# Attention: keys loaded once beside doubled queries, queries asked for ahead of values, first loads moved in memory, bias rows in one transfer

## The chip, the cores and the metric

One core of a Trainium2 chip runs the whole program in one launch. The metric is the device time of a run in microseconds (us), as a median over runs. Engines are named as the profile names them: PE (matmul), PEld (its weight load), DVE (VectorE), ACT (ScalarE), POOL (GpSimd), and SP, which here only starts DMAs. Every engine works through its own instructions in program order, so an instruction that waits holds back all that stand behind it on the same engine.

## The reference, cut to what matters

Two layers of a transformer block over 2048 latent tokens and 256 context tokens, width 1024. In each layer one input projection feeds three head groups: six query heads with two key heads in a window of 128 tokens (called A here), a short convolution, and six heads of two-dimensional neighbourhood attention with a relative position bias (called C). An output projection and a mixture of 16 experts follow. The parts that the change touches are the logits of A and C:

```
s_win = einsum('bnqkgd,bnjkd->bnkgqj', qb, kw) * scale      # A: 384 window keys
s_ctx = einsum('bnqkgd,bjkd->bnkgqj', qb, k_ctx) * scale    # A and C: 256 context keys
s_nb  = einsum('brqhd,brachd->brhqac', qg, kn) * scale      # C: 8 x 64 keys of the grid
s_nb  = s_nb + rpb[:, roff, coff]                           # C: bias by relative position
p = softmax(concat(s_win or s_nb, s_ctx, sink for A))
o = p_win @ v_win + p_ctx @ v_ctx
```

In the second (last) layer the context queries are left out.

## The kernel before, in words

A layer is four stages in a row: `phase_in` (norm, input projection), `phase_att` (A and C), `phase_out` (output projection, norm, router) and `phase_moe`. Matmul operands in float32 are split into a high and a low part; a product is the sum of the products of the parts.

**What phase_in leaves.** It works in five chunks of tokens, 0 to 4; chunk 4 has 256 tokens, the others 512. Each chunk has two tiles `hh` and `hl` of 16 KiB for a partition from the pool `hT` with two buffers of each, so that even and odd chunks alternate. Queries, keys and values go to DRAM as high and low parts (QA, KA, QC, KC: head, part, 64 dimensions, token). The convolution's result goes to DRAM at L725: from SP, and for chunk 4 from POOL.

**How phase_att runs.** Eight units follow one another: A 0 and 1, then C 0 to 5. A unit has blocks of 128 queries for each of its heads: 18 blocks of three steps for A (16 in the last layer), and for C four blocks of four steps, with a fifth of two steps (context) ahead of them in the first layer. The step order is written out by hand: in step i, PE computes the logits of step i (`qk`), DVE adds mask or bias and takes the row maximum of step i-1 (`soft_max`, L1064), ACT takes the exponential (`soft_exp`, L1072), and PE transposes the probabilities of step i-3, which ACT and DVE split (L1201, L1192). A block's products with the values (`pv`) are spread over later steps.

**The logits before.** A query tile holds the high part on partitions 0 to 63 and the low part on 64 to 127, loaded in one DMA. The keys have two tiles: `k0` with the high part in both halves, `k1` with the low part in both, so four DMAs of 64 partitions for a unit (L948). Two matmuls of 128 rows, one with each key tile, add up all four products:

```
for x, k in enumerate((kh, kl)):
    if win: P.matmul(pl[:, w0:512], q, win(k), start=(x == 0), stop=(x == 1))
    P.matmul(pl[:, 512:768], q, k[:, 0:256], start=(x == 0), stop=(x == 1))
```

**Who loads what, and when.** All these loads are on SP. At the first step of block `at`, `qk` calls `load_block` for blocks up to at+2: queries (L973 for A, L981 for C), and for C the window's values `vw` in four DMAs (L986). A `vw` tile is one of three, so that of block at+2 waits until the products of block at-1 are done. `load_unit` for the next unit comes at the unit's fifth block (A) or second block (C). Finished blocks are written to DRAM from SP (L1174, L1180); those of the very last block from POOL. For C, `load_unit` also starts 16 DMAs on POOL (L962), which fetch the shifted bias rows `toep`; POOL subtracts them from the mask (L1004).

**Memory.** Pools are laid one behind the other in the order in which they are opened, and the next stage's pools take the same memory. Counted from the end of the constants, in KiB for a partition: in phase_in `in_x` 0 to 20 and `hT` 20 to 84 (`hh` of even chunks 20 to 36, of odd ones 36 to 52; `hl` of even ones 52 to 68, of odd ones 68 to 84). In phase_att `at_k` 0 to 36, `at_q` 36 to 58.5 (the A queries at its start), `at_s`, `at_p`, `at_h` up to 91.9, `at_o` (finished blocks) 91.9 to 97.9, then `at_w`, `at_v`, `at_b`. In phase_out one small tile and then `out_sb`, from 1.1 to about 80.6, with `mix` first (loaded at L1258), and behind it `out_rows`, whose first load is the row `m2` (L1247; the profile calls these rows m).

Of the kernel before, what the change touches and what calls it, by code (L numbers as in the profile page):

```python
# [12 lines left out]
ALU = mybir.AluOpType  # L13
# [211 lines left out]
def build(ctx, tc, t, out):  # L225
# [279 lines left out]
    def phase_in(l):  # L505
# [5 lines left out]
        hT = {}  # L511
# [102 lines left out]
        def gemm(c):  # L614
# [52 lines left out]
            def b_rest(what, j, pg):  # L667
# [41 lines left out]
                if what == "b":  # L709
# [185 lines left out]
    def phase_att(l):  # L895
        es = ExitStack()
        kp = es.enter_context(tc.tile_pool(name="at_k", bufs=2))
        qp = es.enter_context(tc.tile_pool(name="at_q", bufs=3))
# [3 lines left out]
        op = es.enter_context(tc.tile_pool(name="at_o", bufs=6))  # L902
        wp = es.enter_context(tc.tile_pool(name="at_w", bufs=2))
        vp = es.enter_context(tc.tile_pool(name="at_v", bufs=2))
# [7 lines left out]
        maskA = bp.tile([128, 640 + 512], F32, name="maskA")  # L912
# [16 lines left out]

        def load_unit(kind, u):  # L930
            r = units[kind, u] = {}
            src = (KA if kind == "A" else KC)[l][u]
            ks = r["k"] = [kp.tile([128, TT], F32R, name=f"k{a}") for a in range(2)]
            vs = VS[l].rearrange("(i p) h d -> p i h d", p=128)
            if kind == "A":
                r["v"] = v = vp.tile([128, NT, 128], F32R, name="va")

            pieces = ((0, 5), (5, NT)) if not blks else ((0, NT),)
            first = not blks
            if first:  # L940
                load_block(blist[0])
            for t0, t1 in pieces:
                if first and t0:
                    for b in blist[1:3]:
                        load_block(b)
                for a in range(2):
                    for b in range(2):
                        SY.dma_start(ks[a].bitcast(F32)[64 * b:64 * b + 64, 128 * t0:128 * t1],  # L948
                                     src[a][:, 128 * t0:128 * t1])
                if t0 == 0 and len(pieces) > 1:  # L950
                    SY.dma_start(maskA, t["maskA"])
                if kind == "A":
                    SY.dma_start(v.bitcast(F32)[:, t0:t1], vs[:, t0:t1, u, :])
            if kind == "C":
                v = vp.tile([128, 2, 128], F32R, name="vx")
                SY.dma_start(v.bitcast(F32), vs[:, 0:2, 2 + u, :])
                r["v"] = v
                tz = bp.tile([128, 16, 48], F32, name="toep", bufs=2)
                rp = t["rpb"][l, u]
                tv = tz.rearrange("(a b) i j -> a b i j", a=8)  # L960
# [5 lines left out]
        def load_block(b):  # L966
            kind, u, n = b
            if b in blks:
                return
            r = blks[b] = {}  # L970
            if kind == "A":
                r["q"] = qp.tile([128, 3, 128], F32R, name="qa")
                SY.dma_start(r["q"].bitcast(F32), QA[l][3 * u:3 * u + 3, :, :, 128 * n:128 * n + 128].rearrange(  # L973
                    "m a d n -> (a d) m n"))
                return
            r["q"] = q = qp.tile([128, 4, 128], F32R, name="qc")
            src = QC[l][u].rearrange("a d n -> (a d) n")
            if n == 4:
                SY.dma_start(q.bitcast(F32)[:, 0:2], src[:, 0:256].rearrange("p (m q) -> p m q", m=2))
                return  # L980
            SY.dma_start(q.bitcast(F32).rearrange("p m (h q) -> p (m h) q", h=2),  # L981
                         src[:, 256:].rearrange("p (m g q) -> p m g q", m=8, g=4)[:, :, n, :])
            r["vw"] = vw = qp.tile([128, 8, 128], F32R, name="vw")
            vsr = VS[l][256:TT, 2 + u, :].rearrange("(r a c) d -> a c r d", a=4, c=64)
            for a in range(4):
                SY.dma_start(vw.bitcast(F32)[32 * a:32 * a + 32], vsr[a, CG0[n]:CG0[n] + 32])  # L986

        def bias_part(u, ct, rt):
# [8 lines left out]
            if rt == 0:  # L997
# [8 lines left out]
                            tz[:, i0:i0 + n, j0:j0 + 32], op=ALU.subtract)  # L1006

        loaded = [0]

        def qk(i):  # L1010
            b, m, nm = mem[i]
            kind, u, n = b
            if m == 0:
# [13 lines left out]
            kh, kl = units[kind, u]["k"]  # L1027
            q = blks[b]["q"][:, m, :]
# [936 lines left out]
```

## Time and profile before

| | us |
|---|---|
| median of three runs (4169.72 to 4181.32) | 4175.27 |
| the profiled execution | 4169.93 |
| its span, first to last instruction | 4168.1 |
| phase_att of the first layer: A, then C | 624.7 to 839.2 to 1061.7 |
| phase_att of the second layer: A, then C | 2734.6 to 2928.0 to 3160.6 |

The bounds of a stage are its first and last logits on PE. The profile is one execution, and it lies 5.3 us below the median of the runs. Its idle times belong to the engine named: idle time before an instruction, and behind an arrow what ended it.

### The profile page before, as it was taken

To read this page: it belongs to the slowest core of one execution; us is meant where nothing else is said; L and a number is where in the kernel's file an instruction comes from. 1 tells how busy PE (TensorE), PEld (TensorE's weight loads), DVE (VectorE), ACT (ScalarE), POOL (GpSimd) and SP (SyncE) were. 2 spreads that over 40 slices of the span, in tenths; PEclk is the share of its full clock that TensorE was granted. 3 is DMA by queue.
4 is the path that set the end of the run, shared out by engine and by line. 5 is a ranking of instruction groups with operands and counts; after the bars stand their busy time and mean duration, and the time that the engine had idled before them with its cause. 6 is when DMAs were issued, how large, how long until landed. Compare 5 with 4: busy or idle time off the path is not lost. (4 is left out here: it accounts for less than half of the span.)

```text
span 4168.1 us, 64121 instructions
## 1 busy us (share of the span) xinstructions
PE 3816.9 (92%) x22980; PEld 3252.6 (78%) x22980; DVE 2906.3 (70%) x5836; ACT 2007.4 (48%) x3918; POOL 826.0 (20%) x850
## 2 busy tenths in 40 slices
PE   7999998999998899999997999989989975999983
PEld 5877777888787388989876888778887864999972
DVE  6555557999677477777747765479886776777765
ACT  4344337988433044444424433368775332444453
POOL 0000000144132023323311000011441220222214
PEclk9999998999998999999998999999999986999996
DMA  7566665388643777777766766663786433888885
GB/s 228 170 215 189 203 179 136 82 183 175 226 158 120 217 238 222 211 212 216 210 180 221 220 196 184 174 161 80 147 166 216 168 125 124 251 253 249 246 243 183
DMA packets 733942, 789.93 MB, mean 190 GB/s; under 512 B 121808, under 2 KB 612952, under 8 KB 729784
## 3 DMA queue, kind: packets, MB, share of 16 engines
q1 hardware_dynamic: 692392, 656.83, 54.1%
q0 software_dynamic: 41232, 129.01, 11.4%
q8 instruction: 182, 2.98, 0.3%
q14 instruction: 136, 1.11, 0.1%
HBM read 607.08 MB, written 178.48 MB: 188 GB/s over the span
## 5 line engine op out<-in xcount | busy, mean ns | idle before, releaser
L178 ACT CAST wh<-wraw 128x1024 fp32r<-128x1024 f32 x636 | 656.4, 1049 | 380.8 <-DMA wraw<-in_w_in 132.2
L186 DVE TENSOR_TENSOR wl<-wraw,wh 128x1024 fp32r<-128x1024 f32 x636 | 751.1, 1215 | 17.6 <-ACT wh L178 17.4
L1192 DVE TENSOR_TENSOR pl<-pt,ph 128x256 fp32r<-128x256 f32 (+2 forms) x792 | 359.9, 494 | 21.3 <-ACT ph L1201 16.8
L1201 ACT CAST ph<-pt 128x256 fp32r<-128x256 f32 (+2 forms) x792 | 309.1, 446 | 96.2 <-PE pt L1089 88.7
L626 PE MATMUL gem<-hh,wh 128*128 128x512 f32 (+1 forms) x960 | 355.1, 370 | 0.0
L627 PE MATMUL gem<-hl,wh 128*128 128x512 f32 (+1 forms) x960 | 353.1, 368 | 0.0
L1072 ACT ACTIVATE p<-lg,mx 128x640 f32<-128x640 f32 (+3 forms) x408 | 331.9, 813 | 40.1 <-DVE mx L1064 38.8
L628 PE MATMUL gem<-hh,wl 128*128 128x512 f32 (+1 forms) x960 | 350.6, 365 | 0.0
L1809 PE MATMUL pu<-xh,wh 128*128 128x288 f32 (+1 forms) x1024 | 304.1, 297 | 7.0 <-DVE sa L1637 7.0
L1809 PE MATMUL pa<-xh,wh 128*128 128x288 f32 (+1 forms) x1024 | 300.5, 293 | 0.7 <-DVE modc L419 0.7
L1811 PE MATMUL pa<-xh,wl 128*128 128x288 f32 (+1 forms) x1024 | 296.7, 290 | 0.8 <-DVE wl L186 0.8
L1811 PE MATMUL pu<-xh,wl 128*128 128x288 f32 (+1 forms) x1024 | 296.2, 289 | 0.0
L1810 PE MATMUL pa<-xl,wh 128*128 128x288 f32 (+1 forms) x1024 | 294.0, 287 | 0.0
L1810 PE MATMUL pu<-xl,wh 128*128 128x288 f32 (+1 forms) x1024 | 293.8, 287 | 0.0
L1548 POOL DMA_INDIRECT xe<-H,ix x80 | 161.7, 2021 | 476.3 <-DVE ix L1543 398.3
L1671 POOL DMA_INDIRECT ACC<-y,ix x62 | 128.8, 2077 | 579.6 <-DVE y L1652 326.9
L1846 PE MATMUL py<-wh,gh 128*128 128x512 f32 x512 | 206.4, 403 | 19.6 <-ACT gh L1639 10.8
L804 PE MATMUL gem<-wh,hh 128*128 128x512 f32 x544 | 221.0, 406 | 0.4 <-ACT hh L595 0.4
L805 PE MATMUL gem<-wl,hh 128*128 128x512 f32 x544 | 217.4, 400 | 1.4 <-DVE wl L186 1.4
L806 PE MATMUL gem<-wh,hl 128*128 128x512 f32 x544 | 217.3, 399 | 0.0
L626 PEld LDWEIGHTS gem<-hh,wh 128*128 128x128 f32 x960 | 182.7, 190 | 31.4
L628 PEld LDWEIGHTS gem<-hh,wl 128*128 128x128 f32 x960 | 182.7, 190 | 31.1
(352 smaller groups left out, 9975.1 us busy)
## 6 DMA issues: line engine op xcount, KB each, us to landing
wraw<-in_w_in SPq DMA_DIRECT2D x160, 512.0 KB
wraw<-in_w_gate SPq DMA_DIRECT2D x128, 512.0 KB
wraw<-in_w_up SPq DMA_DIRECT2D x128, 512.0 KB
wraw<-in_w_down SPq DMA_DIRECT2D x128, 512.0 KB
wraw<-in_w_mod SPq DMA_DIRECT2D x88, 512.0 KB
k<-KC SPq DMA_DIRECT2D x48, 576.0 KB
vw<-VS SPq DMA_DIRECT2D x192, 128.0 KB
VS<-vs SPq DMA_DIRECT2D x36, 512.0 KB
```

Of the source, the lines that this page charges most:

```text
L178: self.nc.scalar.copy(h, self.raw[i])
L186: self.nc.vector.tensor_tensor(e[1], self.raw[i], e[0].bitcast(F32), op=ALU.subtract)
L626: P.matmul(pg[:, t0:nt], wh[:, cs_], hh[:, k, t0:nt], start=(k == 0), stop=False)
L627: P.matmul(pg[:, t0:nt], wh[:, cs_], hl[:, k, t0:nt], start=False, stop=False)
L628: P.matmul(pg[:, t0:nt], wl[:, cs_], hh[:, k, t0:nt], start=False, stop=(k == KD - 1))
L804: P.matmul(pg, hh[:, k, tk], wh[:, cs_], start=(k == 0), stop=False)
L1072: S.activation(p[:, 0:768 - w0], rec["lg"][:, w0:768], AF.Exp, bias=st[b]["mx"][:, m:m + 1], scale=-1.0, accum_out=st[b]["ss"][:, m:m + 1])
L1192: V.tensor_tensor(view(st[b]["pl"]), src, view(st[b]["ph"].bitcast(F32)), op=ALU.subtract)
L1201: S.copy(view(st[b]["ph"]), src)
L1809: P.matmul(pp[f], wh[:, cs_], xh[:, kk, :], start=(kk == 0), stop=False)
L1810: P.matmul(pp[f], wh[:, cs_], xl[:, kk, :], start=False, stop=False)
L1811: P.matmul(pp[f], wl[:, cs_], xh[:, kk, :], start=False, stop=(kk == KD - 1))
```

## The change

The query tile gets a further axis of two: entry 0 holds the high part on both halves of the partitions, entry 1 the low part on partitions 0 to 63 and zeros, written once, on 64 to 127. One key tile has the high part on partitions 0 to 63 and the low part on 64 to 127. The two matmuls now differ in the queries and share the keys; the product low by low is left out. Keys take one DMA for a unit, queries three of 64 partitions for a block.

There are four fixed query tiles, and queries are asked for up to block at+3, ahead of the values, which stay at at+2. The bias rows come in one DMA on SP, 128 partitions of 1008 elements, and POOL reads them with a negative step. The convolution's last results leave from ACT instead of POOL. `hT` gives out one pair of tiles that nobody uses, so that the even and odd chunks change places. The pools of phase_att are opened in another order: `at_k` 0 to 18 KiB, `at_q` to 34, `at_vw` to 46, `at_o` to 52, `at_m` (maskA) to 56.5, `at_v` to 76.5, then the others.

```diff
+        hT = {-1: [hp.tile([128, KD, 512], F32R, name=z) for z in ("hh", "hl")]}
...
-                            (G if c == 4 else SY).dma_start(OB[l][j, :, a, d + r0:d + r1], o.bitcast(F32)[:, r0:r1])
+                            (S if c == 4 else SY).dma_start(OB[l][j, :, a, d + r0:d + r1], o.bitcast(F32)[:, r0:r1])
...
         kp = es.enter_context(tc.tile_pool(name="at_k", bufs=2))
-        qp = es.enter_context(tc.tile_pool(name="at_q", bufs=3))
+        qp = es.enter_context(tc.tile_pool(name="at_q", bufs=1))
+        vwp = es.enter_context(tc.tile_pool(name="at_vw", bufs=3))
+        op = es.enter_context(tc.tile_pool(name="at_o", bufs=6))
+        mp = es.enter_context(tc.tile_pool(name="at_m", bufs=1))
+        vp = es.enter_context(tc.tile_pool(name="at_v", bufs=2))
...
+        qs = [qp.tile([128, 2, 4, 128], F32R, name=f"q{i}") for i in range(4)]
+        for q in qs:
+            G.memset(q.bitcast(F32)[64:128, 1], 0.0)
...
-            ks = r["k"] = [kp.tile([128, TT], F32R, name=f"k{a}") for a in range(2)]
+            src = (KA if kind == "A" else KC)[l][u].rearrange("a d n -> (a d) n")
+            k = r["k"] = kp.tile([128, TT], F32R, name="k")
...
+            for t0, t1 in ((0, 5), (5, NT)) if first else ((0, NT),):
+                if first:
+                    more_queries(1 if t0 == 0 else 4)
+                SY.dma_start(k.bitcast(F32)[:, 128 * t0:128 * t1], src[:, 128 * t0:128 * t1])
+                if first and t0 == 0:
                     SY.dma_start(maskA, t["maskA"])
                 if kind == "A":
                     SY.dma_start(v.bitcast(F32)[:, t0:t1], vs[:, t0:t1, u, :])
...
-                for b in range(16):
-                    G.dma_start(tv[:, b], bass.AP(tensor=rp.tensor, offset=rp.offset + 15 * 64 + 15 - b,
-                                                   ap=[[64, 8], [-64, 16], [1, 48]]))
+                n = 15 * 64 + 48
+                SY.dma_start(tz.rearrange("p i j -> p (i j)")[:, 0:n],
+                             bass.AP(tensor=rp.tensor, offset=rp.offset + 15, ap=[[64, 8], [-1, 16], [1, n]]))
...
+        def load_queries(at):
+            b = blist[at]
+            kind, u, n = b
+            r = blks[b] = {}
+            q = r["q"] = qs[at % 4]
+            for x, a, y in ((0, 0, 0), (0, 1, 0), (1, 0, 1)):
+                dst = q.bitcast(F32)[64 * a:64 * a + 64, x]
+                if kind == "A":
+                    SY.dma_start(dst[:, 0:3], QA[l][3 * u:3 * u + 3, y, :, 128 * n:128 * n + 128].rearrange("m d n -> d m n"))
+                    continue
...
-                while loaded[0] < min(at + 3, len(blist)):
-                    load_block(blist[loaded[0]])
-                    loaded[0] += 1
+                more_queries(at + 4)
+                more_values(at + 3)
...
-            for x, k in enumerate((kh, kl)):
+            for x in range(2):
                 if win:
-                    P.matmul(pl[:, w0:512], q, win(k), start=(x == 0), stop=(x == 1))
-                P.matmul(pl[:, 512:768], q, k[:, 0:256], start=(x == 0), stop=(x == 1))
+                    P.matmul(pl[:, w0:512], q[:, x, m, :], win(k), start=(x == 0), stop=(x == 1))
+                P.matmul(pl[:, 512:768], q[:, x, m, :], k[:, 0:256], start=(x == 0), stop=(x == 1))
```

`load_values` keeps the four `vw` DMAs of `load_block` as they were; `more_queries(n)` and `more_values(n)` call the two functions for all blocks below n that are not yet asked for.

## Rows read from the trace of the kernel before

**Rows 1.** The page's first part: busy us, share, instructions of each engine.
```profile
PE 3816.9 (92%) x22980; PEld 3252.6 (78%) x22980; DVE 2906.3 (70%) x5836; ACT 2007.4 (48%) x3918; POOL 826.0 (20%) x850
```

**Rows 2.** Busy time by stage: PE, PEld, DVE, ACT, POOL, then clock, DMA share, GB/s.
```profile
624.70:839.20 214.50, 196.12 (x1320) 176.91 (x1321) 190.38 (x585) 176.20 (x519) 25.68 (x39) 0.94 0.45 110
839.20:1061.70 222.50, 211.81 (x1533) 186.99 (x1532) 208.05 (x514) 187.55 (x478) 90.16 (x112) 1.00 0.85 179
...
3008.70:3049.40 40.70, 35.90 (x248) 32.81 (x248) 32.91 (x76) 29.71 (x72) 20.37 (x28) 0.92 0.84 169
...
3128.60:3160.60 32.00, 32.00 (x238) 29.24 (x239) 30.10 (x72) 27.54 (x67) 3.33 (x3) 1.00 0.72 201
```

**Rows 3.** Timeline of DVE, first layer's A: start, duration, instruction, idle before it.
```profile
631.64 0.76 DVE L1064 CUSTOM_DVE_ANT_0 lg<-lg,maskA,sinks 128x512 f32<-128x512 f32 x1 [10.09 <-PE lg L1043]
...
647.58 0.89 DVE L1064 CUSTOM_DVE_ANT_0 lg<-lg,maskA,sinks 128x640 f32<-128x640 f32 x1 [4.88 <-PE lg L1043]
...
680.79 0.89 DVE L1064 CUSTOM_DVE_ANT_0 lg<-lg,maskA,sinks 128x640 f32<-128x640 f32 x1 [2.44 <-PE lg L1043]
```

**Rows 4.** Timeline of SP, first loads of phase_att in the first layer.
```profile
620.22 0.37 SPq L973 DMA_DIRECT2D qa<-QA  x1
...
623.17 0.53 SPq L951 DMA_DIRECT2D maskA<-in_maskA  x1
```

**Rows 5.** Waits of SP, 600 to 700 us: total, times, longest.
```profile
SPq L973 <- PE gem L628: 8.5, 1, 8.5
```

**Rows 6.** Timeline of SP, the mask's load in the second layer.
```profile
2732.75 0.53 SPq L951 DMA_DIRECT2D maskA<-in_maskA  x1
```

**Rows 7.** Timeline of DVE, second layer's A.
```profile
2740.90 0.76 DVE L1064 CUSTOM_DVE_ANT_0 lg<-lg,maskA,sinks 128x512 f32<-128x512 f32 x1 [9.84 <-DMA maskA<-in_maskA]
...
2755.97 0.89 DVE L1064 CUSTOM_DVE_ANT_0 lg<-lg,maskA,sinks 128x640 f32<-128x640 f32 x1 [4.05 <-PE lg L1043]
...
2787.34 0.89 DVE L1064 CUSTOM_DVE_ANT_0 lg<-lg,maskA,sinks 128x640 f32<-128x640 f32 x1 [1.68 <-PE lg L1043]
```

**Rows 8.** Timeline of PE, second layer's C: first and last of four waits.
```profile
2968.06 0.66 PE L1042 MATMUL lg<-k,qc 128*128 128x384 f32 x1 [4.49 <-DMA qc<-QC]
...
3089.80 0.66 PE L1042 MATMUL lg<-k,qc 128*128 128x384 f32 x1 [4.36 <-DMA qc<-QC]
```

**Rows 9.** Timeline of SP ahead of the first of them.
```profile
2948.82 1.94 SPq L986 DMA_DIRECT2D vw<-VS  x4
2950.82 2.38 SPq L948 DMA_DIRECT2D k<-KC  x4
...
2954.39 0.43 SPq L981 DMA_DIRECT2D qc<-QC  x1
```

**Rows 10.** Stretches of a C unit, without and with the keys' load (columns of Rows 2).
```profile
2984.00:2992.00 8.00, 8.00 (x61) 7.30 (x61) 7.70 (x19) 7.00 (x18) 1.01 (x1) 1.00 0.45 102
2992.00:3000.00 8.00, 8.00 (x61) 7.26 (x60) 7.91 (x19) 7.09 (x18) 3.32 (x3) 1.00 1.03 230
```

**Rows 11.** The bias rows' DMAs on POOL: issue ns min/median/max, first and last.
```profile
L962 POOL DMA_DIRECT2D toep<-in_rpb x192: 591/593/665, 622.5 to 3096.7; - x192
```

**Rows 12.** Timeline of SP, first loads of phase_out in the first layer.
```profile
1071.86 0.35 SPq L1258 DMA_DIRECT2D mix<-MIXA  x1
...
1077.64 0.33 SPq L1247 DMA_DIRECT2D m<-MODR  x1
```

**Rows 13.** Waits of SP, 1050 to 1100 us.
```profile
SPq L1247 <- DMA MIXC<-o: 2.7, 1, 2.7
SPq L1258 <- DVE o L1172: 1.7, 1, 1.7
```

**Rows 14.** Timeline of PE, its first work in phase_out.
```profile
1074.49 0.88 PE L1281 MATMUL pt<-ident,mix 128*128 128x128 f32 x3 [4.10 <-DMA mix<-MIXA]
```

**Rows 15.** Timeline of SP, first loads of phase_out in the second layer.
```profile
3170.59 0.33 SPq L1258 DMA_DIRECT2D mix<-MIXA  x1
...
3176.69 0.33 SPq L1247 DMA_DIRECT2D m<-MODR  x1
```

More of the change, by code (lines that the diff above doesn't have):

```diff
@@ L909, in phase_att @@
         last = l == DEPTH - 1
-        maskA = bp.tile([128, 640 + 512], F32, name="maskA")
+        maskA = mp.tile([128, 640 + 512], F32, name="maskA")
         maskC = bp.tile([128, 3 * MWID], F32, name="maskC")
@@ L928, in phase_att @@
         ustart = {x: min(j for j, b in enumerate(blist) if b[:2] == x) for x in ulist}
+        qs = [qp.tile([128, 2, 4, 128], F32R, name=f"q{i}") for i in range(4)]
+        for q in qs:
+            G.memset(q.bitcast(F32)[64:128, 1], 0.0)
         def load_unit(kind, u):
             r = units[kind, u] = {}
-            src = (KA if kind == "A" else KC)[l][u]
-            ks = r["k"] = [kp.tile([128, TT], F32R, name=f"k{a}") for a in range(2)]
+            src = (KA if kind == "A" else KC)[l][u].rearrange("a d n -> (a d) n")
+            k = r["k"] = kp.tile([128, TT], F32R, name="k")
             vs = VS[l].rearrange("(i p) h d -> p i h d", p=128)
+            first = loaded[0] == 0
             if kind == "A":
                 r["v"] = v = vp.tile([128, NT, 128], F32R, name="va")
[L938 to L950, printed above, removed]
+            for t0, t1 in ((0, 5), (5, NT)) if first else ((0, NT),):
[3 more added lines that the diff above has]
+                if first and t0 == 0:
                     SY.dma_start(maskA, t["maskA"])
@@ L957, in load_unit @@
                 r["v"] = v
-                tz = bp.tile([128, 16, 48], F32, name="toep", bufs=2)
+                tz = bp.tile([128, 16, 64], F32, name="toep", bufs=2)
                 rp = t["rpb"][l, u]
-                tv = tz.rearrange("(a b) i j -> a b i j", a=8)
-                for b in range(16):
-                    G.dma_start(tv[:, b], bass.AP(tensor=rp.tensor, offset=rp.offset + 15 * 64 + 15 - b,
-                                                   ap=[[64, 8], [-64, 16], [1, 48]]))
+                n = 15 * 64 + 48
@@ new lines, in load_queries @@
+            r = blks[b] = {}
[5 more added lines that the diff above has]
+                    continue
+                src = QC[l][u][y]
+                if n == 4:
+                    SY.dma_start(dst[:, 0:2], src[:, 0:256].rearrange("p (m q) -> p m q", m=2))
+                else:
+                    SY.dma_start(dst.rearrange("p m (h q) -> p (m h) q", h=2),
+                                 src[:, 256:].rearrange("p (m g q) -> p m g q", m=8, g=4)[:, :, n, :])
@@ L984, in load_block, with load_values @@
+        def load_values(at):
+            b = blist[at]
+            kind, u, n = b
+            if kind == "A" or n == 4:
+                return
+            blks[b]["vw"] = vw = vwp.tile([128, 8, 128], F32R, name="vw")
             vsr = VS[l][256:TT, 2 + u, :].rearrange("(r a c) d -> a c r d", a=4, c=64)
@@ L986, in load_block, with more_queries, more_values @@
                 SY.dma_start(vw.bitcast(F32)[32 * a:32 * a + 32], vsr[a, CG0[n]:CG0[n] + 32])
+        loaded = [0, 0]
+        def more_queries(n):
+            while loaded[0] < min(n, len(blist)):
+                load_queries(loaded[0])
+                loaded[0] += 1
+        def more_values(n):
+            while loaded[1] < min(n, len(blist)):
+                load_values(loaded[1])
+                loaded[1] += 1
         def bias_part(u, ct, rt):
@@ L1005, in bias_part @@
                             maskC[:, mo:mo + 32 * n].rearrange("p (i j) -> p i j", j=32),
-                            tz[:, i0:i0 + n, j0:j0 + 32], op=ALU.subtract)
-        loaded = [0]
+                            bass.AP(tensor=tz.tensor, offset=tz[:, 15 - i0:16 - i0, j0:j0 + 32].offset,
+                                    ap=[tz.ap[0], [-64, n], [1, 32]]), op=ALU.subtract)
         def qk(i):
@@ L1026, in qk @@
                     W.open(6, 8)
-            kh, kl = units[kind, u]["k"]
-            q = blks[b]["q"][:, m, :]
+            k = units[kind, u]["k"]
+            q = blks[b]["q"]
             pl = psl.tile([128, 1024], F32, name="lg")
```

19 lines of the change are left out of this document (removed).

## Prediction

> **What bounds the kernel now.** I read the page first, then the busy times by stage, then, inside attention, each engine's idle times, and last SP's own order. The page shows PE busy for 92% of the span [rows 1], but that is a mean over stages. In phase_att DVE sets the pace. In a C unit of the second layer that has no long wait, DVE is busy 30.1 of 32.0 us and PE counts as busy throughout [rows 2]; a row of matmuls waiting for nothing but DVE looks like that. So a matmul or a wait of another engine removed here is worth only what DVE stood idle for. The reader should look for idle DVE, and there are three kinds of it.
>
> The first is the start of A: DVE's first maximum comes at 631.64 after 10.09 us idle, and two later steps find 4.88 and 2.44 us [rows 3]; the second layer has 9.84, 4.05 and 1.68 [rows 7]. The second is at the borders between C units in the second layer: PE waits 4.49 to 4.36 us for a query load, four times [rows 8], and the fifth border is a shorter case of it. A unit with such a wait takes 40.7 us [rows 2]. The third is the start of phase_out, below. C in the first layer, with a fifth block in each unit, is at 208 of 222.5 us [rows 2] and has no long wait.
>
> **Matmuls.** Their number, shapes and row counts stay; the stationary operand changes where before the moving one did. That costs nothing, because each matmul already has its own weight load (22980 of each [rows 1]). PE's arithmetic is no term.
>
> **Start of A.** Here the edit means to let the loads go before the last projection matmul ends, by giving them memory that chunk 4 doesn't use. Does the program wait by tile or by pool? Before, the first query tile lies at 36 KiB, in the `hh` pair of the odd chunks, last read in chunk 3. Yet SP stood 8.5 us with that load, until the last matmul of chunk 4 [rows 5], and issued it at 620.22 [rows 4]. The first `mix` load of phase_out says the same: its memory was only the keys', but it waited for DVE's last `o` at L1172 [rows 13], an instruction on other pools. So a new pool waits for all users of every pool under it. The new `at_q`, 18 to 34 KiB, still lies over `hT` from 20 KiB on, so the first query DMA still waits for the last matmul, and the keys, which alone are free, stand behind it on SP. I price the exchange of the chunks at nothing; if the wait goes by tile, that is a rival below.
>
> What is left is shorter loading. Ahead of the first maximum SP moves 192 KB of queries, 640 of keys and 576 of mask, with 393 KB of bias rows beside them (L962 starts at 622.5 [rows 11]): 1801 KB. The mask took 8.5 us from its issue to DVE's start (623.17 to 631.64 [rows 3, 4]) and 8.15 in the second layer [rows 6, 7]. After, it is 288, 320 and 576, and no bias rows: 1184 KB. In proportion 8.2 x 1184/1801 = 5.4 us. Three query DMAs at about 0.4 us and one of keys at 0.6 (four take 2.38 [rows 9]) put the mask's issue at 620.2 + 1.9 = 622.1, so DVE starts at 627.5: 4.1 us gained. In the second layer the mask is issued at 2732.75; 1 us earlier and with 5.4 us for it, 2740.90 becomes 2737.1: 3.8. Bounds: 0, and the 9.2 us that there would be if only the first logits, some 2 us with their wait, stood between the last matmul and DVE. The second wait is for the rest of the keys: 832 KB instead of 1664, though now behind three query tiles (864 KB). Of 4.88 and 4.05 I take 3.4 and 3.0. The third, behind the second unit's keys, halved: 3.0 (with the 1.5 us that follows it) and 1.9. Together **10.5 us in the first layer and 8.7 in the second**; bounds 0 and 20 each.
>
> POOL's four small memsets come before these loads need them; the write from ACT is followed on ACT only by the first exponential, which waits for DVE longer. Both nothing; without that cover they are under 2 us at one start.
>
> **Unit borders of C, second layer.** Why is the query late? At 2948.82 SP gets its `vw` loads out, which had waited for earlier products, then the next unit's keys, 2.36 MB, and only at 2954.39 the query for the next unit's first block [rows 9]; it lands behind the keys, and PE goes on at 2968.06 [rows 8]. After, the same query is asked for one block earlier, ahead of the `vw` that waits, and so ahead of the keys, which are half. Five borders at 40.1 us on average (200.5 from 2928.1 to 3128.6) against 33.6, which is 16 steps at the last unit's 2.1 us: 32.5 us to be had. What comes late next is the DMA engines: 0.84 of 40.7 us [rows 2] is 34 us of transfer in a unit. The keys save 1.18 MB at 230 GB/s: 5.1 us. The queries add 0.52 MB at the rate of the stretch without keys, 102/0.45 = 227 GB/s: 2.3 us [rows 10]. Bias rows: 2048 short pieces become 128 long ones with 0.13 MB more; taken as nothing. That leaves 31.2 us of transfer in 33.6, just under the pace, so I leave a fifth of the stall in: **26 us**. Bounds: 0 (as late by bandwidth as it was by order) and 32.5.
>
> [...] Query DMAs of 64 partitions carry all the queries now. The transfers in rows 10 mix shapes, and the four key loads there, each of 64 partitions in alternate halves, run with the rest at 230 GB/s. [...] The rows, in which no such transfer stands alone, give the sum above.
>
> **C in the first layer, bias rows, POOL.** DVE is at 94% there; its small waits are on ACT and PE. Nothing gained. POOL loses 16 issues of 0.593 us in each unit [rows 11], and was busy 90 of 222.5 us [rows 2]; no one waits for it. If the negative step doubled its subtractions (108 of about 1 us), it would still be far from bound.
>
> **Start of phase_out.** This is the cost. `out_sb` covers 1.1 to 80.6 KiB. Before, `at_o` lay at 91.9, under `out_rows`; there `m2` waited for the last block's writes to DRAM (MIXC) and went at 1077.64, while `mix` had gone at 1071.86 [rows 12, 13]. After, `at_o` lies at 46 to 52 KiB, under `out_sb`. By the same rule of whole pools `mix` must then wait for those writes: 5.8 us later, and 6.1 in the second layer (3170.59 to 3176.69 [rows 15]). PE waits for `mix` there [rows 14] and is busy without a break afterwards. **11.9 us lost**; bounds 0 and 13.
>
> **Sum.** 10.5 + 8.7 + 26 - 11.9 = 33.3. Against the profiled execution: 4169.9 - 33.3 = 4136.6. That execution lies 5.3 us below the median of the runs, so I add half of it: **4139 us**.
>
> **The rivals.**
> Loads by tile (0.12). If waits go by tile, the first loads start up to 8.5 us earlier and `mix` doesn't wait. For: the layout fits the free tiles to the byte. Against: the two waits of [rows 5, 13]. DVE starts at 622.4, so 5.1 us more in each layer, the 2.5 us left of the second waits too, and 11.9 not lost: 4139 - 24.6 = 4114.
>
> Bandwidth takes over from order (0.20). A second-layer unit's queries, 1.57 MB, take 6.9 us at 227 GB/s. At half that rate they take 6.9 more, and the unit needs 31.2 + 6.9 = 38.1 us of transfer. The five borders then gain 5 x (40.1 - 38.1) = 10 us instead of 26: 4155. [...] For: DMA share 1.03 while keys come in [rows 10]. Against: 0.45 elsewhere.
>
> Queries choke the DMA engines (0.06), the slower side. Same place, harder: at a third of the rate, 76 GB/s, they take 13.8 us more in the second layer and 15.2 in the first (1.73 MB a unit). Units then go by DMA: 45.0 us instead of 40.1, five times, and in the first layer 44.1 (0.85 of 37.1 us now [rows 2], less 5.1, plus 2.5 and 15.2) instead of 37.1, six times. That is 66 us lost against 7.3 gained elsewhere: 4139 + 33 + 59 = 4231. It decides from about 2.3 times the present price on, where losses and the 7.3 us balance.
>
> No effect at the borders (0.07): the query waits for something else there, or a `vw` takes its place. Then 7.3 us remain, 10.5 + 8.7 - 11.9: 4139 + 26 = 4165.
>
> **How the numbers follow.** My forecast has 0.55, its own range 4125 to 4150. The range 4108 to 4160 takes in the rivals at 4114 and 4155 and leaves out the rest. Faster by over 0.3% (12.5 us, about what the runs can tell from no change) holds 0.55, 0.12 and most of 0.20: 0.85. Within 0.3%: 0.09. Slower: 0.06.
>
> **What would show it.** SP's first query load in attention directly after the last projection matmul (by pool) or some 8 us ahead of it (by tile). DVE's first maximum some 7 us after that matmul instead of 11. No PE wait on a query at the borders of C, units near 34 us, clock 1.00 there instead of 0.92. First `mix` load behind the last MIXC write. I am wrong if the borders keep their waits with DMA share near 1, or if `mix` goes as early as now.

## The result, and the profile after

The changed kernel takes 4124.34 us (median of four runs, 4118.59 to 4125.43) against 4172.5: a ratio of 0.9883, 95% interval 0.9869 to 0.9897. Its profiled execution took 4118.59 us, 51.3 less than that of before; I had forecast 33.3 less. Against the forecast of 4139 the median lies 15 us low, just under the forecast's own range (4125 to 4150) and inside the whole one (4108 to 4160). Cut at the marks of the text (last projection matmul, first maximum of a step, last logits, first product of the output projection), the 51.3 us lie here:

| stretch | before | after | gained | forecast |
|---|---|---|---|---|
| A, first layer, from the last projection matmul | 219.98 | 204.77 | 15.2 | 10.5 |
| C, first layer, with its last logits | 221.6 | 220.2 | 1.5 | 0 |
| last logits to first product of the output projection | 15.87 | 19.79 | -3.9 | -5.8 |
| A, second layer | 202.24 | 192.24 | 10.0 | 8.7 |
| C, second layer, with its last logits | 228.6 | 196.9 | 31.7 | 26 |
| last logits to first product, second layer | 16.20 | 19.98 | -3.8 | -6.1 |
| all other stages together | | | 0.6 | 0 |

Second layer's C, by units, in the columns of rows 2 (the last row is a unit of the first layer):

```profile
2938.59:2971.88 33.29, 33.29 (x250) 30.35 (x249) 32.12 (x76) 29.41 (x72) 9.30 (x10) 1.00 0.74 173
2971.88:3005.45 33.57, 33.54 (x250) 30.38 (x249) 32.41 (x77) 29.31 (x72) 9.82 (x10) 1.00 0.80 181
...
898.41:935.98 37.57, 36.13 (x265) 31.87 (x264) 35.21 (x86) 31.61 (x82) 9.93 (x10) 1.00 0.69 167
```

A unit takes 33.3 to 33.6 us where it took 40.7 [rows 2], PE counts as busy throughout, and the granted clock is 1.00 instead of 0.92. The transfer share is what I had wrong: 0.77 of 33.4, some 25.8 us, where I had worked out 31.2.

SP ahead of such a border, in order of time:

```profile
2988.01 1.97 SPq L982 DMA_DIRECT2D q<-QC  x3
2990.09 2.04 SPq L994 DMA_DIRECT2D vw<-VS  x4
2992.18 0.45 SPq L951 DMA_DIRECT2D k<-KC  x1
...
2993.20 0.66 SPq L964 DMA_DIRECT2D toep<-in_rpb  x1
...
2996.87 6.29 SPq L982 DMA_DIRECT2D q<-QC  x3
```

The next unit's first query goes at 2988.01, ahead of the values that wait and of the keys; in rows 9 it stood behind both. PE has no wait on a query any more.

The packets in the two traces say where the transfer went. For the loads of five units in the second layer's C, as time of all 16 DMA engines:

| packets | before, us | after, us |
|---|---|---|
| 9216 bytes: keys, 1280 before, 640 after | 54.9 | 16.8 |
| 256 bytes: queries and finished blocks, 31253 and 40561 | 41.9 | 49.0 |
| bias rows, by unit | 2.1 | 2.3 |
| all packets | 176.5 | 146.4 |

Half the key bytes take less than a third of the time: 215 GB/s in four loads of 64 partitions, 351 in one of 128.

The start of A, on SP, then DVE's first maximum in each layer, then what the DMA engines moved meanwhile (columns of rows 2: clock, share and GB/s come last):

```profile
621.28 1.93 SPq L976 DMA_DIRECT2D q<-QA  x3
623.26 0.60 SPq L951 DMA_DIRECT2D k<-KA  x1
623.90 0.47 SPq L953 DMA_DIRECT2D maskA<-in_maskA  x1
624.41 0.43 SPq L955 DMA_DIRECT2D va<-VS  x1
624.89 8.79 SPq L976 DMA_DIRECT2D q<-QA  x9
```

```profile
631.10 0.76 DVE L1083 CUSTOM_DVE_ANT_0 lg<-lg,maskA,sinks 128x512 f32<-128x512 f32 x1 [8.49 <-DMA maskA<-in_maskA]
...
2723.57 0.76 DVE L1083 CUSTOM_DVE_ANT_0 lg<-lg,maskA,sinks 128x512 f32<-128x512 f32 x1 [8.22 <-PE lg L1062]
```

```profile
623.30:625.30 2.00, 0.00 (x0) 0.00 (x0) 0.00 (x0) 0.00 (x0) 1.87 (x2) 0.98 0.87 226
...
627.30:629.30 2.00, 0.98 (x4) 1.01 (x5) 0.00 (x0) 0.00 (x0) 0.00 (x0) 0.50 0.89 296
629.30:631.30 2.00, 1.07 (x6) 0.77 (x4) 0.20 (x1) 0.00 (x0) 0.00 (x0) 0.50 1.16 250
```

The last projection matmul started at 620.97, so the first query load still waits for it: by pool, as forecast. But the first maximum comes 10.1 us behind that matmul (11.7 before) and not some 7. The first logits even start later than before: 7.4 us behind the matmul (at 628.32) and not 4.8. SP lets values and nine more query loads go right behind the mask: from 626 to 630 the mask's packets of 4608 bytes move 0.59 MB, those of other loads 0.44 MB.

The start of phase_out, on SP and on PE, and SP's waits there:

```profile
1060.39 0.34 SPq L1277 DMA_DIRECT2D mix<-MIXA  x1
```

```profile
1063.62 0.88 PE L1300 MATMUL pt<-ident,mix 128*128 128x128 f32 x3 [8.88 <-DMA ml<-OB]
```

```profile
SPq L1277 <- DMA MIXC<-o: 5.6, 3, 3.8
```

The first `mix` load now waits for the last MIXC write, as forecast, where before it waited for DVE's `o` alone [rows 13]; PE's wait grew from 4.10 [rows 14] to 8.88 us.

### The profile page after: what moved, and what is told of

The parts are those of the page before. It is cut to its first block, busy times and chain, and to the rows that moved or that the text cites. A ratio compares the mean times of both kernels' runs of the same rounds, so it can differ in the third digit from the quotient of the medians.

```text
span 4116.8 us, 64178 instructions
## 1 busy us (share of the span) xinstructions
PE 3801.8 (92%) x22980; PEld 3241.1 (79%) x22980; DVE 2899.2 (70%) x5836; ACT 2007.7 (49%) x3918; POOL 706.6 (17%) x658
## 3 DMA queue, kind: packets, MB, share of 16 engines
q10 hardware_dynamic: 1152, 1.05, 0.1%
## 5 line engine op out<-in xcount | busy, mean ns | idle before, releaser
L186 DVE TENSOR_TENSOR wl<-wraw,wh 128x1024 fp32r<-128x1024 f32 x636 | 751.2, 1216 | 19.2 <-ACT wh L178 18.8
L1828 PE MATMUL pu<-xh,wh 128*128 128x288 f32 (+1 forms) x1024 | 304.6, 297 | 10.1 <-DVE sa L1656 10.1
L1061 PE MATMUL lg<-k,q 128*128 128x384 f32 (+2 forms) x768 | 280.1, 387 | 20.9 <-DMA maskA<-in_maskA 7.4
L1062 PE MATMUL lg<-k,q 128*128 128x256 f32 x816 | 228.3, 286 | 0.4 <-ACT p L1091 0.4
L1865 PE MATMUL py<-wh,gh 128*128 128x512 f32 x512 | 206.5, 403 | 17.3 <-ACT gh L1658 10.1
```

The costliest lines, as they stand in the source:

```text
L186: self.nc.vector.tensor_tensor(e[1], self.raw[i], e[0].bitcast(F32), op=ALU.subtract)
L1061: P.matmul(pl[:, w0:512], q[:, x, m, :], win(k), start=(x == 0), stop=(x == 1))
L1828: P.matmul(pp[f], wh[:, cs_], xh[:, kk, :], start=(kk == 0), stop=False)
```

## The experiments

Times are compared by stretch, profile to profile, where a few us matter; other stages differ by up to 4 us from one profile to the next.

**1. Finished blocks outside out_sb.**

```diff
-        op = es.enter_context(tc.tile_pool(name="at_o", bufs=6))
...
         hp = es.enter_context(tc.tile_pool(name="at_h", bufs=2))
+        op = es.enter_context(tc.tile_pool(name="at_o", bufs=6))
```

> The changed kernel with one edit: the pool of finished blocks, at_o, is opened behind at_h again, so that it no longer lies under out_sb. In the changed kernel 19.97 and 20.15 us pass from the last logits of attention to the first product of the output projection (first and second layer), against 16.05 and 16.37 before. Theory (a new pool waits for every user of every pool under it): the first mix load no longer waits for the last MIXC writes, both stretches go back to 16.0 to 16.4 us, and the kernel gains 7.7 us, to about 4111 as profiled (changed kernel 4118.6). Rival (the longer stretch comes from the loads of OB or from the last blocks' writes being slower behind more query DMAs): nothing changes, 4118 to 4120, and the mix load stays behind MIXC. Attention itself stays as it is by both.

Measured: 15.82 and 15.76 us from the last logits to the first product; 4110.05 us in the median, ratio to before 0.9845 (0.9828 to 0.9861). SP, and its waits:

```profile
1055.14 0.34 SPq L1277 DMA_DIRECT2D mix<-MIXA  x1
...
1061.12 0.33 SPq L1266 DMA_DIRECT2D m<-MODR  x1
```

```profile
SPq L1277 <- DVE o L1191: 1.7, 1, 1.7
```

Both stretches are back to the length of before, and the wait for MIXC has gone from `mix` to `m`, for which PE has no wait. The loss was the place of at_o, 4.0 and 4.2 us (19.79 to 15.82, 19.98 to 15.76).

**2. Without the exchange of chunks.**

```diff
-        hT = {-1: [hp.tile([128, KD, 512], F32R, name=z) for z in ("hh", "hl")]}
+        hT = {}
```

> The changed kernel without the exchange of even and odd chunks in hT. Theory (loads wait by whole pools, and at_q overlaps hT in either order): no change, first query load of attention directly after the last projection matmul (0.3 us behind it, as in the changed kernel), first maximum 10.1 and 9.9 us behind that matmul, time within 3 us of 4118.6. Rival (part of the loads does go by tile): first query load or first keys later than now, first maximum 1 us or more later in each layer.

Measured: 4119.09 us in one run, first maximum 10.4 and 10.1 us behind the matmul. SP's waits:

```profile
SPq L976 <- PE gem L629: 8.3, 1, 8.3
```

The wait is the same (8.1 us in the changed kernel). The exchange is worth nothing while any tile of the new pool lies over hT.

**3 and 4. Order and bytes apart.** The first puts the old order into the changed kernel, the second the new order into the kernel before.

```diff
-                more_queries(at + 4)
+                more_queries(at + 3)
```

> The changed kernel with queries asked for up to block at+2 again instead of at+3, so that the first query of a C unit stands on SP behind the values that wait and behind the next unit's keys; keys stay halved, bias rows in one transfer. Second layer's C took 31.7 us less in the changed kernel than before. Theory (order decides): PE waits at the five unit borders are back. The wait before was 4.4 us on PE, some 6.4 us of a unit; with keys of 1.18 MB less (5.1 us of transfer) it can shrink to 1.3 us of a unit, so 7 to 32 us of loss in second layer's C, I say 12, total about 4131. Rival (bytes decide: the halved keys and the short bias transfers were what made room): no waits at the borders, units of 33.3 us, total 4118 to 4121.

```diff
-                while loaded[0] < min(at + 3, len(blist)):
+                while loaded[0] < min(at + 4, len(blist)):
                     load_block(blist[loaded[0]])
                     loaded[0] += 1
+                while valued[0] < min(at + 3, len(blist)):
+                    load_values(blist[valued[0]])
+                    valued[0] += 1
```

Here the queries of A and C share one tile name with four buffers, to fit.

> The kernel before with the order alone: queries asked for up to block at+3 ahead of the values (four query tiles in place of three), values up to at+2 as they were; keys still loaded twice, queries in one DMA of 128 partitions, bias rows in 16 DMAs from POOL. Second layer's C takes 222.9 us from its first maximum to the first of its last block before, 191.2 in the changed kernel, 195.9 in the changed kernel with the old order. Theory A (order decides, as forecast): nearly all of the stalls go, second layer's C takes 191 to 197, total 25 to 32 us below the kernel before, about 4142. Theory B (bytes decide; the old order cost only 4.7 us where the bytes were fewer): order alone brings about 5, second layer's C 215 to 218, about 4165. In between (either alone is enough, because a query that is asked for early has time, and one behind half the keys nearly has): as A. The start of A and the start of phase_out stay as before by all.

Second layer's C, first maximum to that of its last block:

| | keys twice, bias rows in 16 DMAs | keys once, bias rows in one |
|---|---|---|
| queries up to at+2 | 222.9 (before) | 195.9 (0.9888, 0.9871 to 0.9904) |
| queries up to at+3 | 204.1 (0.9942, 0.9921 to 0.9964) | 191.2 (changed) |

In brackets the ratio of the whole run to before. Bytes alone bring 27.0 of the 31.7 us, order alone 18.8: either does most of it. The old order thus costs the changed kernel 4.7 us there and not 12, and the new order alone lies between the two theories on it. It did more than expected elsewhere: A, which was to stay, is 6.8 and 4.6 us shorter than before. Of that, 4.3 and 2.6 us come where the third wait of [rows 3, 7], on PE a wait for a query (2.7 and 2.5 us), is gone. The new order with the old bytes, by units:

```profile
2996.62:3033.56 36.94, 34.92 (x250) 31.89 (x249) 33.15 (x76) 29.81 (x72) 19.42 (x27) 0.95 0.92 179
...
3068.84:3103.99 35.15, 33.55 (x250) 30.36 (x249) 32.55 (x76) 29.57 (x72) 17.63 (x23) 1.00 0.97 191
```

```profile
PE lg L1051 <- DMA k<-KC: 9.1, 5, 2.0
```

There the engines are busy for 0.92 to 0.97 of 35 to 37 us (34 us of transfer) and PE waits five times for keys, no longer for queries. So what I had put next in line, the DMA engines, does come next where the bytes stay.

**5. Bias rows from POOL again.**

```diff
+                for b in range(16):
+                    G.dma_start(tv[:, b], bass.AP(tensor=rp.tensor, offset=rp.offset + 15 * 64 + 15 - b,
+                                                   ap=[[64, 8], [-64, 16], [1, 48]]))
```

in place of the one DMA on SP, with tiles of 16 x 48 and read forwards.

> The changed kernel with the bias rows fetched by 16 DMAs from POOL again, in rows of 48 numbers, and read forwards. The forecast took the bytes and pieces of this edit as nothing. Theory A (nothing): DMA share in a unit of second layer's C stays at 0.73 to 0.80 of 33.4 us (25.6 us on average), start of A unchanged (first maximum 10.1 and 9.9 us behind the last projection matmul), total 4118.6 within 3. Theory B (the 2048 short pieces of a unit are dear in transfer time: a unit's transfers fell from 33 to 25.6 us, 4.6 us more than keys and queries explain): share near 0.9 in those units, but no waits at the borders, since the queries are asked for early; and at the start of A, where POOL fetches the rows of two units at once, the first maximum 1 to 2 us later and the second wait back with 1 to 4 us, total 4 to 10 us above the changed kernel.

Measured: 4133.98 us, 0.9909 (0.9889 to 0.9928). One unit of the second layer's C and one of the first:

```profile
2990.49:3023.80 33.31, 33.31 (x250) 30.36 (x249) 32.72 (x77) 29.43 (x74) 19.17 (x26) 1.00 1.00 181
...
941.57:983.22 41.65, 37.34 (x265) 33.61 (x263) 37.74 (x86) 31.68 (x81) 18.54 (x25) 0.96 0.79 153
```

In the second layer theory B holds: four units hold 29.4 us of transfer each on average (shares 0.74 to 1.00) instead of 25.8, and no waits. Yet the 3.6 us aren't in the rows' own packets, which take 2.0 us a unit. They are in those of other loads: a packet of 512 bytes takes 42 ns on average instead of 38, one of 256 bytes 22 instead of 19. Why is open. At the start of A nothing moved (10.5 and 9.6 us), against B. What neither had foreseen is the first layer: A 6.3 us and C 8.9 us longer. POOL and DVE in that slow unit:

```profile
945.97 3.22 POOL L1026 TENSOR_TENSOR va<-maskC,toep 128x384 f32<-128x384 f32 x3
949.16 1.00 POOL L1026 TENSOR_TENSOR bias<-maskC,toep 128x384 f32<-128x384 f32 x1
```

```profile
946.42 4.03 DVE L1191 TENSOR_TENSOR o<-o,rs 128x256 f32<-128x256 f32 x1
```

DVE's product, 0.40 to 0.42 us where POOL doesn't subtract beside it, lasted 4.03 and ended as POOL's row of four subtractions did. From 950 to 954 PE then worked for 0.37 us only, and from 954 to 958 the granted clock was 0.59. Five such products, from 745.60 (A) to 988.09, lasted 1.57 to 4.03 us, 13 us more than undisturbed ones; at these places the steps fall 17 us behind the changed kernel's, of which some 4 come back. In the changed kernel, where POOL issues no DMA in attention and most of its subtractions wait for DVE one by one, no such product took over 1.40 us.

**6. First loads in memory that is really free.**

```diff
+        mp = es.enter_context(tc.tile_pool(name="at_m", bufs=1))
-        kp = es.enter_context(tc.tile_pool(name="at_k", bufs=2))
+        kps = [es.enter_context(tc.tile_pool(name="at_k", bufs=1))]
+        q0p = es.enter_context(tc.tile_pool(name="at_q0", bufs=1))
+        kps.append(es.enter_context(tc.tile_pool(name="at_k1", bufs=1)))
...
+        qs = [(qp if i else q0p).tile([128, 2, 4, 128], F32R, name=f"q{i}") for i in range(4)]
...
+            if first:
+                more_queries(1)
             for t0, t1 in ((0, 5), (5, NT)) if first else ((0, NT),):
-                if first:
-                    more_queries(1 if t0 == 0 else 4)
                 SY.dma_start(k.bitcast(F32)[:, 128 * t0:128 * t1], src[:, 128 * t0:128 * t1])
```

> The changed kernel with what the first logits and the first maximum need laid wholly into the memory of in_x (0 to 17.5 KiB: maskA 4.5, the first unit's key tile 9, the first query tile 4), and loaded in the order query, keys, mask, rest of the keys, and only then the other queries and values. in_x is last used well before the last projection matmul, and SP is idle from 613.1 to 621.3 in the changed kernel. Theory (pool rule): SP issues these loads near 613 instead of 621.3, the first logits follow the last projection matmul within 2 us, DVE's first maximum comes about 2.5 us behind that matmul instead of 10.1 and 9.9: 7.5 us gained in each layer, 15 in all, about 4103.5 as profiled, if the second to fourth queries (issued at 621.3 and later, needed some 5 us behind the first logits) are not late; if they are, up to 3 us of it is given back in each layer. Rival (the stretch is set by something else, PSUM banks or DVE's last work of the projection): loads go early but the first maximum stays more than 6 us behind the matmul, gain under 8 us in all.

Measured: 4112.32 us, 0.9855 (0.9839 to 0.9872); first maximum 1.7 and 1.6 us behind the matmul, 8.4 and 8.3 gained, but 3.8 and 4.7 at the thirteenth step. SP, ACT and DVE:

```profile
613.17 2.23 SPq L981 DMA_DIRECT2D q<-QA  x3
615.45 0.60 SPq L953 DMA_DIRECT2D k<-KA  x1
```

```profile
626.91 1.28 ACT L1096 ACT_TABLE_LOAD   x1 [4.71 <-DMA va<-VS]
```

```profile
630.41 0.76 DVE L1088 CUSTOM_DVE_ANT_0 lg<-lg,maskA,sinks 128x512 f32<-128x512 f32 x1 [6.21 <-PE lg L1067]
```

Early loads work (the first maximum as expected), and the loss moves to ACT, whose first exponential, with its table load, starts at 626.9. The row names a load of `va`; in the changed kernel the same table load ends a wait of 3.62 us for the convolution's last write to OB, from a tile of in_sb. The next run decides between the two.

**7. The exponential's tiles over hT as well.**

```diff
         wp = es.enter_context(tc.tile_pool(name="at_w", bufs=2))
+        vp = es.enter_context(tc.tile_pool(name="at_v", bufs=2))
```

(at_v opened here and not ahead of at_s, at_o behind at_h as in run 1, and queries 1 to 3 asked for ahead of the first values.)

> The first loads within in_x's memory, and at_o behind at_h, as in the two runs before, and besides: at_s, at_p and at_h are laid ahead of at_v, so that they lie within the memory of hT, and the second to fourth queries go ahead of the first values. In the run with early loads the first maximum came 1.7 us behind the last projection matmul, but the first exponential only at 626.9, after 4.7 us of waiting: at_p lay over in_sb, whose tiles the convolution's last writes to DRAM were still reading; so 8.4 and 8.3 us gained at the first maximum shrank to 3.8 and 4.7 at the thirteenth step. Theory: with at_p over hT the first exponential follows the first maximum directly, the second wait (6.2 us on DVE) falls to about 1.6, and the 4.6 and 3.6 us stay gained; with 8 us from at_o that makes 24.5 below the changed kernel, about 4094 as profiled. Rival: the values, now behind the queries, or the queries themselves come too late for the third to sixth steps, and the second wait stays at 3 us or more; then 4098 to 4102.

Measured: 4096.72 us, 0.9823 (0.9801 to 0.9845), profiled span 4093.1. It was run again beside the changed kernel on one chip, and with one edit more:

> The changed kernel itself, unaltered, beside the two runs after it on the same chip: ratio to the kernel before 0.988 as measured, stretches as in its first profile (first maximum 10 us behind the last projection matmul in both layers, second layer's C 191.2 us, 19.8 and 20.0 us from the last logits to the first product of the output projection).

> The version with the first loads in in_x's memory, at_p and at_h over hT, and at_o outside out_sb, for a closer ratio: 0.982 to the kernel before, 24 us below the changed kernel on the same chip. If the gains at the two starts were given back further on, it would be within 10 us of the changed kernel.

| same chip | median us | ratio to before |
|---|---|---|
| before | 4173.35 | |
| changed kernel | 4121.22 | 0.9876 (0.9861 to 0.9891) |
| run 7 again | 4095.02 | 0.9813 (0.9800 to 0.9827) |
| run 7 with bias rows ahead of keys | 4100.90 | 0.9827 (0.9812 to 0.9841) |

Run 7 again, DVE and ACT at the start of A:

```profile
620.85 0.76 DVE L1088 CUSTOM_DVE_ANT_0 lg<-lg,maskA,sinks 128x512 f32<-128x512 f32 x1
...
624.97 0.76 DVE L1088 CUSTOM_DVE_ANT_0 lg<-lg,maskA,sinks 128x512 f32<-128x512 f32 x1 [2.63 <-PE lg L1067]
```

```profile
621.47 1.28 ACT L1096 ACT_TABLE_LOAD   x1 [1.14 <-DVE stl L722]
```

The exponential follows, the wait of 6.21 is 2.63 (1.6 was expected), and the thirteenth step comes 23.5 and 23.4 us behind the matmul, against 31.4 and 32.4 in the changed kernel. `va` now goes later still (625.43), so it was the memory under at_p, not `va`. This version is faster than both kernels, 26.2 us below the changed one where 24 were expected, and the two intervals don't meet.

**8. Bias rows ahead of the keys.**

```diff
+            if kind == "C":
...
+                SY.dma_start(tz.rearrange("p i j -> p (i j)")[:, 0:n],
+                             bass.AP(tensor=rp.tensor, offset=rp.offset + 15, ap=[[64, 8], [-1, 16], [1, n]]))
...
             for t0, t1 in ((0, 5), (5, NT)) if first else ((0, NT),):
                 SY.dma_start(k.bitcast(F32)[:, 128 * t0:128 * t1], src[:, 128 * t0:128 * t1])
```

> That version with one edit more: the bias rows of the next unit are asked for ahead of its keys, not behind them. In its first profile DVE waited 1.78 us for POOL's bias at the last unit border of the second layer, and that unit took 34.9 us against 33.3. Theory (the bias rows land late behind 1.18 MB of keys): that wait goes and the second layer's C falls from 192.2 to about 190.8, 1 to 2 us in all. Rival (POOL is late for another reason, or the keys become late instead): 192 and above.

Measured: units of 33.3, 34.2, 35.9 and 35.9 us, 198.5 from the first maximum to that of the last block. Of PE's waits in second layer's C:

```profile
PE lg L1066 <- DMA k<-KC: 2.3, 1, 2.3
```

The rival's time holds (192 and above). PE waits at two borders, here for the keys, at the other 2.4 us for nothing that the profile names; that the keys become late instead is shown at one border. The wait of 1.78 us that gave the idea did not come back when run 7 was repeated (units up to 33.4 us).

**9 and 10. Queries loaded twice.** The two DMAs of the high parts of a C block are issued twice; then the same with the bias rows ahead of the keys, as in 8.

```diff
+                    for d in (dst, qd[at % 4].bitcast(F32)[64 * a:64 * a + 64])[0:2 - x]:
+                        SY.dma_start(d.rearrange("p m (h q) -> p (m h) q", h=2),
```

> The changed kernel with the two DMAs of a C block's high parts (64 partitions each, 128 KB each) made twice, the second time into tiles that nobody reads: 1.05 MB more in a unit. Price as forecast (227 GB/s over the 16 engines): 4.6 us more transfer in a unit of second layer's C, share up from 0.77 to about 0.90, no waits at the borders, total 4118 to 4123. Rival (a DMA of 64 partitions moves at half that rate): 9.2 us more, 34.8 us of transfer in 33.4, so the units stretch to 35 us and more, share at 0.97 and above, total 4128 to 4140. [...]

> The run with doubled query loads again, with the bias rows asked for ahead of the keys. There the second layer's C took 217.2 us instead of 191.2, with units of 36.7 to 41.4 us at a DMA share of only 0.78 to 0.88, and DVE waited 6.2 to 8.1 us at the borders for POOL, which waited for the bias rows. Theory (not the rate of the transfers but the place of the bias rows behind the keys is what the added loads make late): waits at the borders shrink to under 3 us, second layer's C 193 to 205. Rival (loads of 64 partitions are so slow that the engines cannot keep the pace): the time stays lost, keys or queries are late in place of the bias rows, second layer's C at 213 and above.

Measured: 4163.64 and 4178.29 us, one run each; second layer's C 217.2 us in the first, units of 36.7 to 41.4 us, 226.0 us and units of 40.0 to 42.5 us in the second. The first run is slower than both of its prices, at a share under both of them; the second reaches the rival's time (213 and above) without the rival's cause. The first run, a unit, DVE's wait in it, and SP:

```profile
2995.13:3036.55 41.42, 36.18 (x242) 33.04 (x243) 32.17 (x76) 29.18 (x72) 9.77 (x10) 0.90 0.78 174
```

```profile
3036.55 0.83 DVE L1085 CUSTOM_DVE_ANT_0 lg<-lg,bias 128x640 f32<-128x640 f32 x1 [7.30 <-POOL bias L1027]
```

```profile
3000.00 0.62 SPq L984 DMA_DIRECT2D q<-QC  x1
...
3023.36 0.45 SPq L952 DMA_DIRECT2D k<-KC  x1
...
3024.39 0.65 SPq L965 DMA_DIRECT2D toep<-in_rpb  x1
```

The second run, PE:

```profile
3043.82 0.66 PE L1063 MATMUL lg<-k,q 128*128 128x384 f32 x1 [6.41 <-DMA k<-KC]
```

The engines aren't full: 0.78 of 41.4 is 32.3 us of transfer, 6.5 more for 1.05 MB: 161 GB/s, between the two prices, if the other loads took no longer than without it. SP is: from 3000.00 to 3027 it issues almost without a gap, each query DMA 0.62 us, and reaches the keys 28.2 us after the unit's start, where it reaches them 20.3 us after it in the changed kernel (2992.18 against 2971.88). There its 47 issues already take up 31.8 of 33.6 us, waits among them; before, 42 issues took 24.5 of 40.7. Whatever then stands last on SP is late: the bias rows, or, with those moved ahead, the keys. How much of the delay is SP's issuing and how much the slower landing stays open; other queues for the queries weren't tried.

## Why the prediction was right, and where it was off

The direction and every place were right: DVE sets the pace, the borders of the second layer's C carry most of the gain, the starts of A the rest, and phase_out gives some back. That DVE and not PE sets the pace where nothing else waits (DVE busy 32.1 of 33.3 us, PE throughout) is argued; no run changed the work of either. All four sizes were off: three gains too low, the loss too high. The four errors add up to 16 us in one direction.

- **Matmuls, nothing.** Holds: in C's units, PE is busy throughout and 249 weight loads stand beside 250 matmuls.
- **By pool, not by tile.** Right, by runs 1, 2 and 6: the same edit with memory of in_x alone brings the first load 8 us forward, and the exchange of chunks alone brings nothing. The rival at 4114 falls; run 7, which does what that rival assumed, comes in at 4095.
- **First maximum, 4.1 and 3.8 forecast, 1.6 in both.** The step that failed is the loading time of the mask, 5.4 us by the proportion of bytes: it took 7.2 and 6.9 us from its issue to the maximum. It was also issued some 0.7 us later than forecast: the three query DMAs took 1.93 us and not 1.2. I counted the 1184 KB asked for ahead of the mask. From 623.3 on the DMA engines run at 0.84 to 1.16 share, and in the 10 us from the first issue to the maximum they move some 2.0 MB, values and later queries among them. That this company made the mask late is argued; no run took it away alone.
- **Second and third waits, 3.4 + 3.0 and 3.0 + 1.9 forecast.** From the first maximum to the thirteenth step 8.3 and 5.1 us were gained, to the twenty-fifth 4.4 and 2.6 more. The waits went wholly, and with them what I had left out: the slower steps behind each. One of them, the third, goes by the order alone as well (run 4), and not only by the halved keys. Before, PE stood 3.97 us ahead of 646.67 (first layer), and the granted clock then was 0.50 until about 652, with DVE waiting twice more, 1.16 and 1.14 us, for ACT behind PE. In the trace of before, PE and then the columns of rows 2:

```profile
646.67 0.66 PE L1042 MATMUL lg<-k,qa 128*128 128x384 f32 x1 [3.97 <-DMA k<-KA]
```

```profile
646.60:649.20 2.60, 2.53 (x10) 2.47 (x11) 0.95 (x2) 0.02 (x1) 0.00 (x0) 0.50 0.37 105
649.20:652.00 2.80, 2.80 (x12) 2.51 (x11) 1.85 (x5) 1.56 (x4) 0.00 (x0) 0.50 0.01 3
652.00:655.00 3.00, 3.00 (x23) 2.76 (x22) 2.08 (x6) 2.74 (x9) 0.00 (x0) 0.99 0.20 60
```

  From the seventh step, which ends that wait, to the ninth the gain grows from 7.5 to 10.0 us. This more than made up for the first maximum: that A came out as near its forecast as it did is luck, two errors of opposite sign.
- **Unit borders, 26 forecast, 31.7.** The mechanism holds; the size was held down by 31.2 us of transfer, of which there are 25.8. Three terms of that sum were mis-sized. The start, 34 us, is that of the unit with the highest share; in the four units from 2969.61 on it is 0.78 to 0.85, 32.5 us on average. The keys saved 7.6 us a unit (54.9 to 16.8 in five) and not 5.1. The packets of 256 bytes cost 1.4 more, where the queries were to cost 2.3. That is 4.9 of the 5.4 us. The bias rows, "taken as nothing", are nothing by their own packets; fetched from POOL they do make other loads slower in the changed kernel, by 3.6 us a unit (run 5). Nor was order the one cause: bytes alone bring 27.0, order alone 18.8.
- **C of the first layer, POOL, nothing.** 1.5 us gained, and run 5 shows that the bias edit isn't free there: undone, it costs 15 us, 6.3 of them in A, with products of DVE that last up to 4.03 us beside POOL's subtractions. The kernel before, with the same 16 DMAs, had one product of 3.20 us and one of 1.81 there.
- **Start of phase_out, 5.8 and 6.1 forecast, 3.9 and 3.8.** Right in kind (run 1), too large: I took the whole distance from `mix` to `m2` before, where the last MIXC write had to land beside six other loads. Now nothing is loaded beside it, and `mix` goes 4.3 us after DVE's last `o`. Run 1, where the six loads go beside the write again, has 6.1 us from that `o` to `m` (5.9 before). That the company of loads makes the difference fits both, but nothing else was held apart.
- **Rivals.** Bandwidth takes over: true of run 4's bytes, not of the change. That queries in loads of 64 partitions move at half the rate, as the rival at 4155 supposed, is shown by no run: a packet of 256 bytes takes 21 ns before, with queries in loads of 128 partitions, and 19 after, in loads of 64. The keys moved at 215 GB/s in loads of 64 partitions and at 351 in one of 128, which speaks for the edit; whether the form or the doubled bytes made the difference isn't held apart. The added loads of run 9 moved at 161 GB/s, between the 227 that I took and its half, and at a share of 0.77 it decides nothing. The choke happens at twice the high parts' loads, not through the engines but, as far as run 9 shows, through SP.

## What to carry to other kernels

Memory given to a stage's first loads helped here only where all users of every pool under the new pool were done (first maximum 8.4 and 8.3 us earlier in run 6, no gain by the exchange in run 2): lay the few tiles of the first step in a pool of their own over memory that is free early, and look at every first writer (loads, first exponential, first store), because the next one took over the wait here (4.71 us on ACT in run 6). Of the stall at the borders, caused by order and by bytes together, either cure took most (18.8 and 27.0 us), and both together 31.7, less than their gains added. Before adding DMAs to a queue, add up its issue times in a unit of work: in run 9 a queue with almost no gap was late with whatever it issued last, at a DMA share of 0.78.

## What the runs showed of the hardware

A DVE product (`o` by `rs`, 128x256), 0.40 to 0.42 us undisturbed, took 4.03 us beside four subtractions of POOL in a row (run 5): it started at 946.42, 0.45 us behind the first of them, and ended at 950.45, 0.29 us behind the last. That POOL held it up, with all four and not with one, is argued from these times.

Starting a query load of 128 KB took SP 0.62 us in run 9, and with eight more of them in a unit that took 33.3 us without them, SP has almost no gap from 3000.00 to 3027, at a DMA share of 0.78 in the unit. Here that time is scarce.
